# In-projection of a hybrid decoder layer: the column halves six k-steps apart, the woven steps spread evenly, the samples' states multiplied eight at a time

## The chip, the cores and the metric

The kernel runs on one core of a Trainium2 chip. The metric is the device time of one execution in microseconds (us). Its engines have a queue each and run them in order: TensorE (PE in the profile) multiplies, VectorE (DVE), ScalarE (ACT) and GpSimd (POOL) work on elements, SyncE (SP) issues most of the transfers.

## The reference

One step of a one-layer decoder with 520 token columns (512 of a prompt, 8 single new tokens, the samples) of width 2048:

```python
h = h + W_out [ GatedDeltaNet(x_n) ; MultiScalePool(x_n) ]     # x_n = RMSNorm(h)
h = h + SwiGLU(RMSNorm(h))
# W_in: 2048 -> [q | k | v | z | beta | decay | pool channels], q, k, v, z, pool 1024 wide each
def short_conv(buf, x, w):
    ext = jnp.concatenate([buf.astype(x.dtype), x], axis=1)
    T = x.shape[1]
    y = ext[:, 0:T] * w[0]
    for i in range(1, CONV_W):
        y = y + ext[:, i:i + T] * w[i]
    return jax.nn.silu(y), ext[:, -(CONV_W - 1):]
```

q, k and v go through the short convolution. The delta net has 8 heads of dimension 128: for the prompt its recurrence is computed in chunks, and each sample reads and updates its own state, a 128 x 128 matrix per head (`state_delta`, 8 samples x 8 heads). The second half of the width is pooled over windows of 2, 4, 8 and 16 tokens. Everything is float32.

## The kernel before, in words

The change lies in the first stage, the in-projection with the delta net and the pooling, up to about 580 us. The rest (out-projection and the feed-forward part) is not touched.

**Products.** `product` (L171 to L194 and its `step`) computes 128 output columns of W_in for all 520 tokens. There are 16 k-steps of 128 rows. Each float32 operand is split into two parts, hi and lo, and three matmuls stand for one: hi by hi (L171), hi by lo of the activations (L172), lo of the weights by hi (L173). The 520 tokens lie in two halves of 264 and 256 with an accumulator (mm) each, from a pool of three. So a product is 16 x 2 x 3 = 96 matmuls. Half 1 runs `SKEW` = 3 k-steps behind half 0: nine matmuls of half 0 alone, then both halves in turn, then nine of half 1 alone. As soon as a half is done it is evicted (by VectorE, L263 with the norm's factor), which frees its buffer for the next product.

**Weights.** A product's weights come in two granules of eight k-steps (512 KB). For each there is a load on SyncE's queue (raw, L134), the high part by ScalarE (hi, L138) and the low part by VectorE (lo, L140); three buffers of each serve in turn, so a granule can be split when the product before the last has read its own. These have a high priority in the queues, as have the evictions; apart from PE, whose order is that of the program (`manual_schedule`), a scheduler sets the order of the instructions on the engines.

**The weave.** The heads' own work (`keys`, `eliminate`, `delta`, `gate`, and the samples' and the pooling's steps) is cut into pieces by `yield n`: a generator yields after a piece, and runs on after n steps of the weave. `product` calls `weave.step()` 16 times. Before, there is none in the nine first matmuls; then one for every six matmuls, and in the last nine one for every three. So a piece is put in PE's queue between the product's matmuls, and what PE reads there has to be ready, or PE's whole queue waits.

**A head.** `delta` (two products per head, q and v) multiplies with a stored triangle (L871), does three elimination steps (L881 on PE, the result uu by VectorE in L883, the transposed factor xt_ by ScalarE in L873), and then four chunks in a chain: R from the state S (kp by PE in L908, R by VectorE in L910), W from R (L915), the new state S (L920 on PE; L923 or L925 on VectorE). The squares of queries and outputs are taken by ScalarE (L797, L934), the convolution y by VectorE (L748, L750). `eliminate` is a chain of 62 operations on VectorE for four heads at a time. The order of the products: four k tiles, four z tiles, and for each of four heads q and v; the same for the next four heads; then eight tiles of the pooling channels. The gates z are evicted into mixa and mixb.

**The samples.** In `sample_product` (L1000 on), a piece per four samples of a head: their states (s0, 256 KB, two buffers in turn, L1006 on SyncE's queue) are loaded, four matmuls multiply them with the key and query columns, each into its own 32 rows of one accumulator (L1009), and after four steps of the weave the next four follow: sixteen groups of four, in the products of the third to the last but one pool tile. The pieces of `sample_out` stand behind them (L1020, L1040, L1048).

Of the kernel before, what the change touches and what calls it, by code (L numbers as in the profile page):

```python
# [17 lines left out]
P = 128  # L18
D = 2048
KT = D // P  # L20
# [3 lines left out]
H = 8  # L24
# [11 lines left out]
    "ext": 2, "y": 1, "ys": 1, "g3": 3, "junk": 1, "ss": 2, "rr": 2, "nb": 1, "u": 1, "tm": 2, "xt_": 1, "uu": 2,  # L36
    "qts": 1, "fq": 2, "aq": 1, "vs": 1, "bt": 2, "tq": 1, "R": 2, "W": 2, "S": 2, "so": 2, "ro": 2, "s0": 2, "s2": 1, "kd": 4, "st": 2,
}
SKEW = 3
AHEAD = 2000  # L40


# [27 lines left out]
def decoder_kernel(ctx, tc, x_prompt, x_sample, state_delta, state_conv, state_pool, norm_mix, w_in,  # L70
# [4 lines left out]
    te, act, dve, pool, sp = nc.tensor, nc.scalar, nc.vector, nc.gpsimd, nc.sync  # L75
# [12 lines left out]
    def pst():  # L88
        return ps_dn.tile([P, 512], F32, tag="dn", name="dn")
# [34 lines left out]
    weave = Weave()  # L124
# [27 lines left out]
    def weights(view, K, parts=None):  # L152

        ng = -(-K // HG)
        sizes = [K // ng + (1 if i < K % ng else 0) for i in range(ng)]
        out = []
        k0 = 0
        for n in sizes:
            hi, lo = granule(view, k0, n, P, parts)
            for j in range(n):  # L160
                out.append((hi[:, j, :], lo[:, j, :]))
            k0 += n
        return out

    def accumulators():
        return [ps_mm.tile([P, c1 - c0], F32, tag="mm", name="mm") for c0, c1 in CHUNKS]

    def step(acc, w, hi, lo, ci, k):
        c0, c1 = CHUNKS[ci]
        wh, wl = w[k]  # L170
        te.matmul(acc[ci], wh, hi[k][:, c0:c1], start=(k == 0), stop=False)  # L171
        te.matmul(acc[ci], wh, lo[k][:, c0:c1], start=False, stop=False)  # L172
        te.matmul(acc[ci], wl, hi[k][:, c0:c1], start=False, stop=(k == len(w) - 1))  # L173

    def product(w, hi, lo, evict, skew=SKEW):

        K = len(w)
        acc = accumulators()

        def finish(ci):  # L180
            with tc.high_priority(offset=AHEAD):
                evict(ci, *CHUNKS[ci], acc[ci])

        for i in range(K + skew):
            if i < K:
                step(acc, w, hi, lo, 0, i)
                if i == K - 1:
                    finish(0)
            if i >= skew:
                step(acc, w, hi, lo, 1, i - skew)  # L190
                if i < K + skew - 1:
                    weave.step()
        finish(1)
        weave.step()  # L194

    def split(hi, lo, src):
        act.copy(hi, src)
        dve.tensor_tensor(lo, src, hi.bitcast(F32), op=ALU.subtract)  # L198
# [82 lines left out]
    with tc.tile_pool(name="ph0", bufs=2) as ph0, tc.high_priority(offset=10 * AHEAD), tc.manual_schedule():  # L281
# [173 lines left out]
        for i in range(17):  # L455
# [53 lines left out]
            ci, j = divmod(i, 8)  # L509
# [31 lines left out]
    with ExitStack() as p1:  # L541
# [4 lines left out]
        def d1tile(tag, shape, name, dtype=F32):  # L546
            return (pre if tag == "ext" else d1).tile(shape, dtype, tag=tag, name=name, bufs=BUFS[tag])
# [193 lines left out]
        def qkv_tile(sec, h, out, ext=None):  # L741
            t = sec * 8 + h
            if ext is None:
                ext = columns()
                product(weights(win_view(sec * 1024 + h * P), KT), xhk, xlk,
                        lambda ci, c0, c1, acc: to_columns(ext, t, ci, acc))
            y = d1tile("y", [P, SEQ], "y")
            dve.tensor_scalar(y, ext[:, 0:SEQ], cw(0, t), None, op0=ALU.mult)  # L748
            for i in range(1, 4):
                dve.scalar_tensor_tensor(y, ext[:, i:i + SEQ], cw(i, t), y, op0=ALU.mult, op1=ALU.add)  # L750
            act.activation(out, y, AF.Silu)
            pool.tensor_copy(ccp[:, :, t], ext[:, SEQ:SEQ + 3])
# [206 lines left out]
        smp = {}  # L959
# [40 lines left out]
        def sample_product(h):  # L1000

            if h == 0:
                smp["pk"] = pst()
            for hf in range(2):
                s0 = d1tile("uu", [P, 4, P], "s0")
                sp.dma_start(s0, state_delta[0, 4 * hf:4 * hf + 4, h].rearrange("b k v -> k b v"))  # L1006
                i = 2 * h + hf
                for j in range(4):
                    te.matmul(smp["pk"][32 * j:32 * j + 32, 0:P], smp["cols"][j][:, 32 * i:32 * i + 32], s0[:, j, :],  # L1009
                              start=(i == 0), stop=(i == 2 * H - 1))  # L1010
                yield 4

        def sample_out():
            take = smp["take"]
# [56 lines left out]
        def z_tile(h):  # L1071
            w = weights(win_view(3072 + h * P), KT)

            def evict(ci, c0, c1, acc):
                normed_out(mix[h][:, c0:c1], acc, c0, c1, c0)
                act.activation(mix[h][:, c0:c1], mix[h][:, c0:c1], AF.Silu)

            product(w, xhk, xlk, evict)
# [4 lines left out]
        def pool_tile(t, operands):  # L1083
# [6 lines left out]
            def evict(ci, c0, c1, acc):  # L1090
# [3 lines left out]
                else:  # L1094
                    normed_out(pe0[:, 15 + 256:15 + 512], acc, 264, NTOK, 264)

            product(w, xhk, xlk, evict)
            pool.tensor_copy(pcp[:, :, t], pe0[:, 512:527])
            cur = pe0
# [73 lines left out]
        for h in range(H):  # L1173
            weave.add(sample_product(h))
# [19 lines left out]
        order = [*range(8), 14, 15, 12, 13, 10, 11, 8, 9]  # L1194
# [3 lines left out]
        w = weights(w_out[0].rearrange("(k p) c -> p k c", p=P)[:, :, 8 * P:9 * P], KT)  # L1198
        acc_out = [ps_mm.tile([P, HALF], F32, tag="mm", name="mm") for _ in range(3)]

        def step_out(i, half):
            k = order[i]
            (wh, wl), c = w[k], slice(HALF * half, HALF * half + HALF)
            acc = acc_out[2 if half else k // 8]
            start, stop = i == 0 or not half and i == 8, i == KT - 1 or not half and i == 7
            te.matmul(acc, wh, xhk[k][:, c], start=start, stop=False)
            te.matmul(acc, wh, xlk[k][:, c], start=False, stop=False)
            te.matmul(acc, wl, xhk[k][:, c], start=False, stop=stop)

        for i in range(KT + SKEW):  # L1210
            if i == 14:
                weave.finish(1)
                for k in order[14:]:
                    split(xhk[k], xlk[k], mix[k])
            if i < KT:
                step_out(i, 0)
            if i >= SKEW:
                step_out(i - SKEW, 1)
            weave.step()
        mixed_t3 = mixed(2, 8), mixed(0, 2)  # L1220

# [438 lines left out]
    w = last.w  # L1660
# [32 lines left out]
    def add_to(i, half, acc):  # L1693
        x = mix[KT - 2 + i][:, HALF * half:HALF * half + HALF]
        dve.tensor_tensor(x, x, acc, op=ALU.add)

    def finish(i, half, acc):
        c = slice(HALF * half, HALF * half + HALF)
        add_to(i, half, acc)
        sq = p2.tile([P, NTOK], F32, tag="sq", name="sq")[:, c]  # L1700
        act.activation(sq, mix[KT - 2 + i][:, c], AF.Square)
        act.dma_start(h_d[KT - 2 + i][:, c], mix[KT - 2 + i][:, c])
        return sq, c
# [534 lines left out]
```

## Time and profile before

| | |
|---|---|
| median of 3 runs | 2142.9 us (2142.05 to 2143.71) |
| profiled execution | 2141.42 us, its span 2139.7 us |
| clock granted to TensorE over the span | 0.999 |
| TensorE busy | 2113.0 us |
| VectorE busy | 1774.5 us |
| ScalarE busy | 931.3 us |
| GpSimd busy | 434.9 us |

A row of the timeline gives start and duration in us, the engine, the line, the operation, output and inputs with their shapes, the number of instructions that it joins, and in brackets how long the engine stood idle before it and on what. Matmuls are pipelined: one lasts 0.28 us from start to end, but the next starts 0.12 us after it, so distances are taken between starts. In the waits, a row gives the engine and its line, the engine and line it waited for, the total in us, how often, and the longest. Start times in the text are those of the profiled execution, counted from the span's start. Places in a product are counted in its matmuls, of which there are 96.

### The profile page before, as it was taken

To read this page: it belongs to the slowest core of one execution; us is meant where nothing else is said; L and a number is where in the kernel's file an instruction comes from. 1 tells how busy PE (TensorE), PEld (TensorE's weight loads), DVE (VectorE), ACT (ScalarE), POOL (GpSimd) and SP (SyncE) were. 2 spreads that over 40 slices of the span, in tenths; PEclk is the share of its full clock that TensorE was granted. 3 is DMA by queue.
4 is the path that set the end of the run, shared out by engine and by line. 5 is a ranking of instruction groups with operands and counts; after the bars stand their busy time and mean duration, and the time that the engine had idled before them with its cause. 6 is when DMAs were issued, how large, how long until landed. Compare 5 with 4: busy or idle time off the path is not lost.

```text
span 2139.7 us, 42813 instructions
## 1 busy us (share of the span) xinstructions
PE 2113.0 (99%) x17685; PEld 2095.2 (98%) x17685; DVE 1774.5 (83%) x2616; ACT 931.3 (44%) x1369; POOL 434.9 (20%) x524
## 2 busy tenths in 40 slices
PE   8999999999999999999999999999999999999998
PEld 7999999999999999999999999999999999999998
DVE  7786767676699979888889889888877888888997
ACT  5533452442354454434334434434334434435444
POOL 2212320232012202332233233231011101001100
PEclk9999999999999999999999999999999999999999
DMA  8344434444445524655555656555448648348333
GB/s 277 101 129 107 122 98 122 116 112 111 129 133 159 162 87 131 175 179 173 168 173 176 181 168 182 144 145 152 122 127 249 192 134 261 106 120 267 90 108 120
DMA packets 477488, 321.29 MB, mean 150 GB/s; under 512 B 27692, under 2 KB 455365, under 8 KB 476765
## 3 DMA queue, kind: packets, MB, share of 16 engines
q1 hardware_dynamic: 459965, 263.49, 43.0%
q0 software_dynamic: 16016, 54.25, 7.9%
q8 instruction: 139, 2.28, 0.5%
q10 hardware_dynamic: 1312, 0.80, 0.1%
q14 instruction: 56, 0.46, 0.1%
HBM read 265.76 MB, written 53.40 MB: 149 GB/s over the span
## 4 chain that ended last, share of the span: by engine, by line
PE 85%; DVE 9%; issue 2%; ACT 2%; DMA 1%; POOL 1%; ACTq 0%; DVEq 0%; POOLq 0%; SPq 0%
PE dn L1280 21%; PE dn L1281 21%; PE dn L1282 21%; PE mm L171 6%; PE mm L173 5%; PE mm L172 5%; DVE lo L1274 1%; DVE lo L140 1%; PE dn L881 1%; ACT hi L1273 1%; DVE raw L1316 1%; DMA qk<-tok_d 1%; DVE xl L198 0%; DVE tm L847 0%; DVE u L849 0%
## 5 line engine op out<-in xcount | busy, mean ns | idle before, releaser
L1274 DVE TENSOR_TENSOR lo<-raw,hi 128x1024 fp32r<-128x1024 f32 (+1 forms) x422 | 543.2, 1307 | 70.3 <-ACT hi L1273 68.8
L1273 ACT CAST hi<-raw 128x1024 fp32r<-128x1024 f32 (+1 forms) x422 | 426.8, 1027 | 401.0 <-DVE raw L1316 226.5
L171 PE MATMUL mm<-xh,hi 128*128 128x256 f32 (+1 forms) x1280 | 376.7, 294 | 2.5 <-DVE mixa L263 2.5
L172 PE MATMUL mm<-xl,hi 128*128 128x256 f32 (+1 forms) x1280 | 361.6, 283 | 0.9 <-DVE xl L354 0.5
L173 PE MATMUL mm<-xh,lo 128*128 128x256 f32 (+1 forms) x1280 | 361.7, 283 | 0.4 <-DVE lo L140 0.4
L171 PEld LDWEIGHTS mm<-xh,hi 128*128 128x128 f32 x1280 | 241.1, 188 | 6.8 <-DVE mixa L263 3.2
L172 PEld LDWEIGHTS mm<-xl,hi 128*128 128x128 f32 x1280 | 241.6, 189 | 1.7 <-DVE xl L354 1.7
L173 PEld LDWEIGHTS mm<-xh,lo 128*128 128x128 f32 x1280 | 240.8, 188 | 0.6 <-DVE lo L140 0.6
L1282 PE MATMUL dn<-b21h,lo 128*128 128x260 f32 x598 | 169.3, 283 | 0.4 <-DVE lo L1274 0.4
L1281 PE MATMUL dn<-b21l,hi 128*128 128x260 f32 x598 | 169.4, 283 | 0.0
L1280 PE MATMUL dn<-b21h,hi 128*128 128x260 f32 x598 | 168.7, 282 | 0.0
L1282 PE MATMUL dn<-b11h,lo 128*128 128x260 f32 x590 | 167.0, 283 | 1.3 <-DVE lo L1274 1.3
L1316 DVE TENSOR_TENSOR raw<-raw 128x1024 f32<-128x1024 f32 (+1 forms) x130 | 166.2, 1278 | 2.2
L1281 PE MATMUL dn<-b11l,hi 128*128 128x260 f32 x590 | 167.1, 283 | 0.0
L1280 PE MATMUL dn<-b11h,hi 128*128 128x260 f32 x590 | 166.6, 282 | 0.0
L1486 POOL TENSOR_TENSOR mixa<-mixa 128x520 f32<-128x520 f32 x22 | 50.4, 2290 | 568.7 <-DVE mixa L1480 568.7
L1467 ACT ACTIVATE sg<-sg 128x260 f32<-128x260 f32 x88 | 37.0, 422 | 264.9 <-DVE sg L1466 264.9
L1280 PE MATMUL dn<-T1h,hi 128*128 128x260 f32 x534 | 151.9, 284 | 0.0
L1281 PE MATMUL dn<-T1l,hi 128*128 128x260 f32 x534 | 151.5, 284 | 0.0
L138 ACT CAST hi<-raw 128x1024 fp32r<-128x1024 f32 (+2 forms) x86 | 87.2, 1015 | 142.3 <-PE mm L172 135.4
L140 DVE TENSOR_TENSOR lo<-raw,hi 128x1024 fp32r<-128x1024 f32 (+2 forms) x87 | 102.1, 1175 | 52.9 <-ACT hi L138 51.4
L1282 PE MATMUL dn<-T1h,lo 128*128 128x260 f32 x512 | 144.3, 282 | 0.0
(671 smaller groups left out, 6695.3 us busy)
## 6 DMA issues: line engine op xcount, KB each, us to landing
raw<-in_w_gate_up_dram SPq DMA_DIRECT2D x134, 512.0 KB
raw<-in_w_in_dram SPq DMA_DIRECT2D x79, 512.0 KB
a_d<-mixa SPq DMA_DIRECT2D x22, 1040.0 KB
raw<-in_w_down_dram SPq DMA_DIRECT2D x48, 448.0 KB
mixb<-in_w_gate_up_dram SPq DMA_DIRECT2D x41, 512.0 KB
raw<-in_w_out_dram SPq DMA_DIRECT2D x25, 512.0 KB
raw<-in_w_down_dram SPq DMA_DIRECT2D x24, 512.0 KB
sg<-in_w_down_dram SPq DMA_DIRECT2D x14, 448.0 KB
```

The lines of the kernel that those rows point to most:

```text
L138: act.copy(hi[:, r], raw[:, r])
L140: dve.tensor_tensor(lo[:, r], raw[:, r], hi[:, r].bitcast(F32), op=ALU.subtract)
L171: te.matmul(acc[ci], wh, hi[k][:, c0:c1], start=(k == 0), stop=False)
L172: te.matmul(acc[ci], wh, lo[k][:, c0:c1], start=False, stop=False)
L173: te.matmul(acc[ci], wl, hi[k][:, c0:c1], start=False, stop=(k == len(w) - 1))
L1273: act.copy(hi, raw)
L1274: dve.tensor_tensor(lo, raw, hi.bitcast(F32), op=ALU.subtract)
L1280: te.matmul(acc, wh[:, k, :], xf[:, k, :], start=start and k == 0, stop=False)
L1281: te.matmul(acc, wh[:, k, :], xg[:, k, :], start=False, stop=False)
L1282: te.matmul(acc, wl[:, k, :], xf[:, k, :], start=False, stop=stop and k == wh.shape[1] - 1)
L1316: dve.tensor_tensor(r[name], r[a], r[b], op=op)
L1486: pool.tensor_tensor(q[:, 4:8:2, :], q[:, 1:4:2, :], q[:, 0:2, :], op=ALU.subtract)
```

## The change

Three things are changed, all in the in-projection. `SKEW` goes from 3 to 6: half 1 of each product runs six k-steps behind half 0, so that 18 matmuls of half 0 stand alone at the start and 18 of half 1 at the end. The weave's steps no longer hang on half 1's k-steps: the product's 32 pairs of half and k-step are written as one list, and every second of them is followed by a step, so one for every six matmuls from matmul 6 to 96; there are 16 as before. The samples' states are loaded for a whole head at a time, two tiles of four samples, and multiplied in one group of eight; the group comes every eight steps (after six the first time), and the next head's loads are issued behind it. The out-projection's own loop used the same constant and keeps 3 (`lag`).

```diff
-SKEW = 3
+SKEW = 6
...
-        for i in range(K + skew):
-            if i < K:
-                step(acc, w, hi, lo, 0, i)
-                if i == K - 1:
-                    finish(0)
-            if i >= skew:
-                step(acc, w, hi, lo, 1, i - skew)
-                if i < K + skew - 1:
-                    weave.step()
-        finish(1)
-        weave.step()
+        order = [(ci, i - skew * ci) for i in range(K + skew) for ci in range(2) if 0 <= i - skew * ci < K]
+        for n, (ci, k) in enumerate(order):
+            step(acc, w, hi, lo, ci, k)
+            if k == K - 1:
+                finish(ci)
+            if n % 2:
+                weave.step()
...
             if h == 0:
                 smp["pk"] = pst()
+                load_states(0)
+                yield 6
+            for hf in range(2):
+                i = 2 * h + hf
+                for j in range(4):
+                    te.matmul(smp["pk"][32 * j:32 * j + 32, 0:P], smp["cols"][j][:, 32 * i:32 * i + 32],
+                              smp["s0"][hf][:, j, :], start=(i == 0), stop=(i == 2 * H - 1))
+            if h + 1 < H:
+                load_states(h + 1)
+                yield 8
+
+        def load_states(h):
+            smp["s0"] = []
             for hf in range(2):
                 s0 = d1tile("uu", [P, 4, P], "s0")
                 sp.dma_start(s0, state_delta[0, 4 * hf:4 * hf + 4, h].rearrange("b k v -> k b v"))
-                i = 2 * h + hf
-                for j in range(4):
-                    te.matmul(smp["pk"][32 * j:32 * j + 32, 0:P], smp["cols"][j][:, 32 * i:32 * i + 32], s0[:, j, :],
-                              start=(i == 0), stop=(i == 2 * H - 1))
-                yield 4
+                smp["s0"].append(s0)
```

The lines of the changed kernel stand four lower in the part that matters (L881 becomes L877, L915 becomes L911, the states' L1009 becomes L1005, their load L1006 becomes L1015).

More of the change, by code (lines that the diff above doesn't have):

```diff
@@ L1208, in step_out @@
             te.matmul(acc, wl, xhk[k][:, c], start=False, stop=stop)
-        for i in range(KT + SKEW):
+        lag = 3
+        for i in range(KT + lag):
             if i == 14:
@@ L1216, in decoder_kernel @@
                 step_out(i, 0)
-            if i >= SKEW:
-                step_out(i - SKEW, 1)
+            if i >= lag:
+                step_out(i - lag, 1)
             weave.step()
```

## The prediction

> **What bounds it now.** First the page's busy times and its chain of waits:
>
> ```profile
> PE 2113.0 (99%) x17685; PEld 2095.2 (98%) x17685; DVE 1774.5 (83%) x2616; ACT 931.3 (44%) x1369; POOL 434.9 (20%) x524
> PE 85%; DVE 9%; issue 2%; ACT 2%; DMA 1%; POOL 1%; ACTq 0%; DVEq 0%; POOLq 0%; SPq 0%
> ```
>
> PE (TensorE) has work 99% of the time and carries 85% of the chain. The change leaves the number of its matmuls as it is, so it can win only where PE stands still or pays for a switch, and lose only where PE gets a new wait. Next the busy time by stage of the in-projection, and PE's waits from 60 to 606 us:
>
> ```profile
> core 0: us, PE busy (x) PEld busy (x) DVE busy (x) ACT busy (x) POOL busy (x), PEclk, DMA share, GB/s
> 100.00:160.00 60.00, 57.18 (x471) 56.34 (x469) 50.24 (x122) 19.70 (x33) 10.74 (x23) 1.00 0.48 125
> 160.00:500.00 340.00, 338.40 (x2912) 335.13 (x2913) 235.30 (x537) 136.91 (x302) 83.31 (x163) 1.00 0.41 111
> 570.00:606.00 36.00, 34.88 (x289) 34.42 (x288) 30.43 (x65) 18.77 (x33) 1.53 (x3) 1.00 0.31 88
> ```
> ```profile
> engine line waited for: us in total, times, longest us
> PE mm L171 <- DVE mixa L263: 2.5, 3, 1.2
> PE dn L881 <- DVE uu L883: 0.7, 1, 0.7
> PE dn L881 <- ACT xt__2114 L873: 0.7, 1, 0.7
> PE dn L881 <- ACT xt__4928 L873: 0.5, 1, 0.5
> PE dn L1040 <- DVE sc_u L1037: 0.3, 1, 0.3
> ```
>
> The clock is 1.00 in every stage. There is little to win: 2.5 us in three z products, where the next product needs the accumulator that VectorE has not yet read, 1.9 us in three elimination steps of a head, and 0.3 us near the end. The long stage with the heads, 160 to 500, has 1.6 us of idle PE in 340, though VectorE is busy for 235: the weave already fits, with little slack at each place, as the rows below show.
>
> **The sample's states.** Now a group of four states:
>
> ```profile
> 514.08 0.28 PE L173 MATMUL mm<-xh,lo 128*128 128x256 f32 x1
> 514.28 0.42 PE L1009 MATMUL dn<-s,utf 128*32 128x128 f32 x8
> 514.64 0.39 PE L171 MATMUL mm<-xh,hi 128*128 128x264 f32 x1
> 514.87 0.29 PE L172 MATMUL mm<-xl,hi 128*128 128x264 f32 x1
> 514.99 0.29 PE L173 MATMUL mm<-xh,lo 128*128 128x264 f32 x1
> ```
>
> From L173 to L173 there are 0.91 us; the product's own three starts, 0.12 apart (514.87 to 514.99), would take 0.36, so a group adds 0.55. It is two sets of four side by side. Eight states are two sets more in the same group, each about 0.135: 0.36 from the group's start to L171 is two sets and the way out, and the way out is taken at 0.09, which leaves 0.135 for a set. So a group of eight adds 0.55 + 0.27 = 0.82, and eight of these in place of sixteen of 0.55 give 8 x (1.10 - 0.82) = **-2.2 us** (bounds -3.3, if the added sets cost nothing, to 0, if each pair of groups costs as much as before).
>
> **Its loads.** The pair of tiles for the next head can be loaded only when the whole group has read the last pair; before, one of the two was always under way. On SyncE's queue, around the sixth pool tile (s0 are the states, raw the weight granules of the seventh and eighth pool tile), stood:
>
> ```order
> L134 DMA raw_6982<-in_w_pool_dram 128x2x256
> L1006 DMA s0_6805<-in_state_delta_dram 128x4x128
> L1006 DMA s0_6837<-in_state_delta_dram 128x4x128
> L1006 DMA s0_6898<-in_state_delta_dram 128x4x128
> L134 DMA raw_7060<-in_w_in_dram 128x8x128
> L134 DMA raw_7066<-in_w_in_dram 128x8x128
> L1006 DMA s0_6928<-in_state_delta_dram 128x4x128
> ```
>
> and now
>
> ```order
> L1015 DMA s0_6716<-in_state_delta_dram 128x4x128
> L1015 DMA s0_6718<-in_state_delta_dram 128x4x128
> L134 DMA raw_7058<-in_w_in_dram 128x8x128
> L1015 DMA s0_6814<-in_state_delta_dram 128x4x128
> L134 DMA raw_7064<-in_w_in_dram 128x8x128
> L1015 DMA s0_6816<-in_state_delta_dram 128x4x128
> ```
>
> The second half of head 3's pair stands behind both weight loads, each of which waits until VectorE has split an earlier granule. The same four transfers in the trace of before, and the traffic from 531 to 539 in slices of 0.2 us:
>
> ```profile
> 531.40 0.37 SPq L1006 DMA_DIRECT2D s<-in_state_delta_dram  x1
> 531.83 1.68 SPq L134 DMA_DIRECT2D raw<-in_w_in_dram  x2
> 534.84 0.37 SPq L1006 DMA_DIRECT2D s<-in_state_delta_dram  x1
> GB/s 0 0 0 0 0 0 0 118 136 77 261 343 336 277 328 333 335 320 348 364 289 287 284 261 292 297 307 294 302 300 292 302 282 253 184 85 21 0 0 10
> ```
>
> 1.5 MB (256, 512, 512 and 256 KB) flow at about 300 GB/s until 538, 6.6 us after the first issue. In the changed kernel all four are issued from 2.3 us after matmul 66 of the fourth pool tile, where the split of the granule begins (a hi and a lo, rows below), and are through at 2.3 + 6.6 = 8.9; the next group stands 48 matmuls behind the group at that place: 0.82 + 48 x 0.12 = 6.6, and its second half 0.4 later. PE would wait 8.9 - 7.0 = 1.9 us, once; at the other pairs nothing stands between. I take **+1.6** (0 if the last transfer overtakes, 2.4 if it lands last of all). The Trainium skill, page DMA: Bandwidth & Descriptors, section Anatomy of one DMA, gives a transfer as some 2.0 us fixed and bytes over 436 GB/s; by that the four would take 5.6 us and the wait would be an estimated 0.9 us. The traffic above stays at about 300, so the rows decide.
>
> **Later accumulators.** Half 0 now ends at matmul 75 of 96 instead of 84, and the next product asks for its buffer at 21 instead of 12: 42 matmuls, 5.0 us, in place of 24, 2.9 us. The three waits on mixa end there. But between 100 and 160 VectorE is busy 50 of 60 us with the elimination, whose chain has to be through for the first head; what z no longer waits for is waited for there. **+0.5** (-2.5, all of the waits gone, to +2).
>
> Weights: granule 1's buffer comes free at matmul 66 instead of 57 and the next product reads it from 30 instead of 39: 60 matmuls, 7.2 us, for a hi of 1.05 and a lo of 1.23 us (rows below). Hidden: 0.
>
> **The weave nine matmuls earlier.** Before, the first step came after matmul 15, now after 6; at most places of a head that is 9 x 0.12 = 1.08 us earlier in the product. VectorE's queue isn't earlier by that. For one head, the first elimination step's result and the step that reads it:
>
> ```profile
> 225.16 0.55 DVE L883 SCALAR_TENSOR_TENSOR uu<-dn,utf 96x384 f32<-96x384 f32 x1
> 226.11 0.27 PE L881 MATMUL dn<-uu,xt__2900 128*64 128x64 f32 x1
> ```
>
> uu is there at 225.71, behind a queue of VectorE that runs without a pause; PE comes to it at 226.11 and would now come at 225.03: a wait of 0.68. **A**: five heads (1, 2, 3, 5, 6) x 0.65 = **+3.2** (0 to 5, if the queue is ahead by then or if the signal takes 0.2 more). Heads 4 and 7 hold two of the three waits on L881 and get a queue in another order: **-0.6** (-1.3 to +1).
>
> The next place is the second chunk of a head. VectorE's queue before (S the state, lo the weights' low part, ext and ccs the eviction, R the right side that PE multiplies in L915, y the convolution):
>
> ```order
> L140 TENSOR_TENSOR lo_2686<-raw_2684,hi_2685 128x1024
> L955 SCALAR_TENSOR_TENSOR mixa_100<-mixb_101,prm_105,mixa_100 128x512
> L923 COPY S_2616<-dn_2614 128x128
> L910 SCALAR_TENSOR_TENSOR R_2637<-dn_2635,negc_668,vs_2561 128x128
> L263 TENSOR_TENSOR ext_2456<-mm_2470,rb_113 128x256
> L263 TENSOR_TENSOR ccs_112<-mm_2470,rb_113 128x8
> L263 TENSOR_TENSOR ext_2456<-mm_2471,rb_113 128x256
> L925 SCALAR_TENSOR_TENSOR S_2663<-S_2616,egl_670,dn_2661 128x128
> L748 TENSOR_SCALAR y_2668<-ext_2456,prm_105 128x512
> L140 TENSOR_TENSOR lo_2857<-raw_2855,hi_2856 128x1024
> L750 SCALAR_TENSOR_TENSOR y_2668<-ext_2456,prm_105,y_2668 128x512
> L910 SCALAR_TENSOR_TENSOR R_2709<-dn_2707,negc_668,vs_2561 128x128
> ```
>
> and now:
>
> ```order
> L919 COPY S_2607<-dn_2605 128x128
> L140 TENSOR_TENSOR lo_2686<-raw_2684,hi_2685 128x1024
> L259 TENSOR_TENSOR ext_2456<-mm_2470,rb_113 128x256
> L259 TENSOR_TENSOR ccs_112<-mm_2470,rb_113 128x8
> L906 SCALAR_TENSOR_TENSOR R_2628<-dn_2626,negc_668,vs_2552 128x128
> L951 SCALAR_TENSOR_TENSOR mixa_100<-mixb_101,prm_105,mixa_100 128x512
> L259 TENSOR_TENSOR ext_2456<-mm_2471,rb_113 128x256
> L921 SCALAR_TENSOR_TENSOR S_2663<-S_2607,egl_670,dn_2661 128x128
> L744 TENSOR_SCALAR y_2668<-ext_2456,prm_105 128x512
> L140 TENSOR_TENSOR lo_2857<-raw_2855,hi_2856 128x1024
> L746 SCALAR_TENSOR_TENSOR y_2668<-ext_2456,prm_105,y_2668 128x512
> L906 SCALAR_TENSOR_TENSOR R_2700<-dn_2698,negc_668,vs_2552 128x128
> ```
>
> The first R now has the weights' lo and the eviction between it and S; the second R keeps its place behind lo and y. Their times in before, on ScalarE, VectorE and PE:
>
> ```profile
> 230.03 1.05 ACT L138 CAST hi<-raw 128x1024 fp32r<-128x1024 f32 x1 [4.12 <-PE mm L172]
> ```
> ```profile
> 231.12 1.23 DVE L140 TENSOR_TENSOR lo<-raw,hi 128x1024 fp32r<-128x1024 f32 x1 [1.33 <-ACT hi L138]
> 232.26 0.75 DVE L955 SCALAR_TENSOR_TENSOR mixa<-mixb,prm,mixa 128x512 f32<-128x512 f32 x1
> ...
> 233.94 0.35 DVE L910 SCALAR_TENSOR_TENSOR R<-dn,negc,vs 128x128 f32<-128x128 f32 x1 [0.73 <-PE dn L908]
> 234.31 0.42 DVE L263 TENSOR_TENSOR ext<-mm,rb 128x256 f32<-128x256 f32 x1
> 234.65 0.17 DVE L263 TENSOR_TENSOR ccs<-mm,rb 128x8 f32<-128x8 f32 x1
> ...
> 236.94 1.22 DVE L140 TENSOR_TENSOR lo<-raw,hi 128x1024 fp32r<-128x1024 f32 x1
> 238.07 0.75 DVE L750 SCALAR_TENSOR_TENSOR y<-ext,prm,y 128x512 f32<-128x512 f32 x1
> 238.74 0.34 DVE L910 SCALAR_TENSOR_TENSOR R<-dn,negc,vs 128x128 f32<-128x128 f32 x1
> ```
> ```profile
> 234.82 0.38 PE L915 MATMUL dn<-R,uu 128*128 128x128 f32 x2
> 239.88 0.38 PE L915 MATMUL dn<-R,uu 128*128 128x128 f32 x2
> ```
>
> **B**, first R: hi starts when PE lets its buffer go, 9 matmuls later: 231.11. So lo starts at 232.20, ext at 233.34 (1.14 later, as 231.12 to 232.26), ccs 0.34 later, R at 233.82, done at 234.17. PE comes to L915 six matmuls earlier (84 instead of 90), 234.10, and needs some 0.2 for the signal: 0.28, in eight heads **+2.2** (0 to 4). **C**, second R: in the next product everything of VectorE's keeps its distance from the product's start, so R is there at 239.08; L915 comes at 18 instead of 27, 238.80: 0.28 and 0.07 for the signal, in seven heads **+2.5** (0 to 3.5).
>
> **The end.** From 570 to 606 VectorE is busy 30.4 of 36 us; the last sample steps come nine to 21 matmuls earlier, which takes the 0.3 wait on L1040 and a little of the queue behind it: **-0.7** (-1.5 to +1, if the lo of the last pool tile's weights comes late).
>
> **Sum**: -2.2 + 1.6 + 0.5 + 3.2 - 0.6 + 2.2 + 2.5 - 0.7 = +6.5 us. On the profiled execution's 2141.4 that is 2147.9; the median of the runs is 1.5 above it, so 2149.4.
>
> **Rivals.**
> 1. *The queue gives way.* VectorE has 105 idle us in the 340 of the heads; S and the squares come earlier as well, and if the queue gets ahead of PE once, A, B and C are nothing. For it: only a few tenths of a us decide each. Against it: the rows before uu and R stand back to back. Then -2.2 - 2.5 - 0.6 - 0.7 + 0 = -6.0: 2136.9, or with the load's 1.6, 2138.5. Faster; chance 0.27.
> 2. *Half of it.* A alone or B and C alone: 6.5 less 3.2 or 4.7, 2144.7 to 2146.2, no change to be told. Chance 0.27. (The states' loads in time, alone, would leave 6.5 - 1.6 = 4.9, 2147.8, still slower.)
> 3. *Weights late.* If the lo of a granule gets behind two evictions and the pool tile's chain, the window of 7.2 us could be short where pool granules hold a buffer; one such wait of 1 us in each of the last four products would be +4 on the sum, 2153.4. Within the forecast's side; it decides where the window's 7.2 us are less than queue and split.
>
> **Numbers.** Slower by the sum and by rival 3: 0.46. 0.2%, 4.3 us, is about what a measurement of this kernel can tell from no change, so slower begins at 2147.2 and faster ends at 2138.6. The range takes in rival 1's 2136.9 and, upward, A, B and C at 0.9 us more each than taken with rival 3 half true (6.5 + 2.7 + 2 = 11.2, 2154.1): 2136.5 to 2154.5. The forecast's own range is 2147 to 2154.5.
>
> **What would show it.** In the changed kernel's waits: L877 (the old L881) on uu some five times at 0.6, L911 (old L915) on R about fifteen times at 0.3, and L1005 on s0 once at 1 to 2 us; no wait on mixa's eviction; PE's sample groups eight at 0.8 us. Each of the R rows in VectorE's queue should end after PE has come. I am wrong if PE's idle time between 160 and 500 doesn't grow from 1.6 us to some 8; if it shrinks, rival 1 holds.

## The result, and the profile after

The changed kernel takes 2158.69 us (median of 4 runs, 2157.07 to 2160.22) beside 2142.78 for the kernel before: a ratio of 1.0075 (95% interval 1.0062 to 1.0087). It is slower by 16 us, where 6.5 us were forecast. The profiled execution took 2157.3 us, its span is 2155.6.

First the page's busy times and the top of its chain:

```profile
PE 2117.4 (98%) x17685; PEld 2098.6 (97%) x17685; DVE 1771.2 (82%) x2616; ACT 937.6 (43%) x1373; POOL 439.0 (20%) x524
PE 77%; DVE 7%; ACT 2%; issue 1%; DMA 0%; POOL 0%; DVEq 0%; SPq 0%; ACTq 0%; POOLq 0%
```

The work is the same, and VectorE isn't busier than before. The time went into waits. The same stages as in the prediction:

```profile
core 0: us, PE busy (x) PEld busy (x) DVE busy (x) ACT busy (x) POOL busy (x), PEclk, DMA share, GB/s
100.00:160.00 60.00, 56.28 (x453) 55.66 (x452) 46.58 (x122) 23.78 (x31) 7.52 (x18) 0.97 0.42 114
160.00:500.00 340.00, 328.86 (x2797) 322.38 (x2797) 225.86 (x521) 133.78 (x299) 85.85 (x162) 1.00 0.40 109
570.00:606.00 36.00, 36.00 (x332) 34.98 (x331) 27.20 (x59) 13.91 (x22) 0.65 (x4) 1.00 0.45 126
```

In the stretch of the heads, 160 to 500, PE is idle for 11.1 us instead of 1.6, and in 100 to 160 the granted clock is 0.97. PE's waits from 60 to 606 us say for what:

```profile
PE dn L892 <- ACT vT L747: 4.4, 6, 1.5
PE dn L877 <- DVE uu L879: 4.2, 6, 2.8
PE mm L171 <- DVE mixa L259: 3.3, 2, 2.5
PE dn L911 <- DVE R L906: 2.2, 10, 0.3
PE dn L1005 <- DMA s<-in_state_delta_dram: 1.2, 1, 1.2
PE mm L173 <- DVE lo L140: 0.4, 1, 0.4
PE dn L911 <- DVE pw L1116: 0.3, 1, 0.3
```

Only waits of 0.15 us or more are listed. Three of the rows were forecast: uu, R and the states' load. The first was not: the transposition of vT. And mixa's wait, which was to go, grew from three waits of 2.5 in all to two of 3.3. Where the time is lost is best read from the starts of the products, compared with those of before (each from its profiled execution, in us; the products are numbered from 0 and a stretch runs from start to start; the first head, number 0, is multiplied in products 10 and 11, the heads 1 to 3 lie in 11 to 18, the heads 4 to 7 in 26 to 34, the states in 34 to 39):

| stretch | 2 to 11 | 11 to 18 | 18 to 26 | 26 to 34 | 34 to 39 | the rest |
|---|---|---|---|---|---|---|
| forecast | +0.5 | heads together +7.3 | 0 | | -0.6 | -0.7 |
| changed kernel | +5.2 | +6.0 | 0.0 | +5.9 | -2.0 | +0.7 |

The 0.3 us wait on L1040, which the forecast counted to the end (-0.7), lay in product 38, so it belongs to the stretch 34 to 39.

**A head.** In the third head's product, VectorE, ScalarE and PE:

```profile
231.01 0.70 DVE L771 STREAM_TRANSPOSE bt<-mixb 128x512 f32<-128x512 f32 x1
231.64 0.71 DVE L746 SCALAR_TENSOR_TENSOR y<-ext,prm,y 128x512 f32<-128x512 f32 x1
232.27 0.55 DVE L879 SCALAR_TENSOR_TENSOR uu<-dn,utf 96x384 f32<-96x384 f32 x1
232.74 0.74 DVE L746 SCALAR_TENSOR_TENSOR y<-ext,prm,y 128x512 f32<-128x512 f32 x1
```
```profile
233.51 0.63 ACT L747 ACTIVATE vT<-y 128x512 f32<-128x512 f32 x1 [2.33 <-DVE y L746]
```
```profile
232.96 0.65 PE L877 MATMUL dn<-uu,xt__2891 128*64 128x64 f32 x8 [0.26 <-DVE uu L879]
234.19 0.44 PE L892 MATMUL dn<-ident,vT 128*128 128x128 f32 x2 [0.58 <-ACT vT L747]
```

uu now has VectorE before the last pass of the convolution, so it comes earlier than forecast, and PE waits 0.26 for it. But the pass that was put behind it ends at 233.48, the silu at 234.14, and the transposition, which stands in PE's queue right behind L877, waits 0.58. In the kernel before, the same rows had room:

```profile
225.28 0.63 ACT L751 ACTIVATE vT<-y 128x512 f32<-128x512 f32 x1 [1.03 <-DVE y L750]
```
```profile
226.11 0.68 PE L881 MATMUL dn<-uu,xt__2900 128*64 128x64 f32 x8
226.72 0.66 PE L896 MATMUL dn<-ident,vT 128*128 128x128 f32 x4
```

vT was there at 225.91, 0.81 before PE needed it. Two deadlines 0.6 us apart hung on one queue, and the forecast priced one.

**The elimination.** The load of its input nb, behind a weight load on SyncE's queue, and VectorE's first operation of it, before and after:

```profile
108.05 0.40 SPq L134 DMA_DIRECT2D raw<-in_w_in_dram  x1
108.49 0.58 SPq L786 DMA_DIRECT2D gcb<-gcr_d  x1
109.74 0.53 SPq L837 DMA_DIRECT2D nb<-nd_d  x1
```
```profile
113.98 0.20 DVE L847 TENSOR_TENSOR tm<-nb,u 64x31 f32<-64x31 f32 x1 [0.38 <-DMA nb<-nd_d]
```
```profile
109.92 0.37 SPq L782 DMA_DIRECT2D gcb<-gcr_d  x1
110.81 0.41 SPq L134 DMA_DIRECT2D raw<-in_w_in_dram  x1
111.46 0.53 SPq L833 DMA_DIRECT2D nb<-nd_d  x1
```
```profile
117.84 0.20 DVE L843 TENSOR_TENSOR tm<-nb,u 64x31 f32<-64x31 f32 x1 [6.33 <-DMA nb<-nd_d]
```

nb is asked for 1.7 us later and takes 6.4 us instead of 4.2, so VectorE stands idle for 6.3 us and its chain of 62 operations begins 3.9 us late. The rest of it follows from there: z's eviction waits among those operations, and PE for the eviction. In the first head it is again VectorE's queue that passes the delay on. The convolution of its queries follows the elimination there, so their load (qk) is issued at 158.34 instead of 154.21, ScalarE's squares of them come later, and uu stands in the queue behind their sums (ss):

```profile
165.97 0.17 DVE L931 TENSOR_SCALAR ss<-ss 128x4 f32<-128x4 f32 x1 [1.82 <-ACT junk L930]
166.05 0.75 DVE L746 SCALAR_TENSOR_TENSOR y<-ext,prm,y 128x512 f32<-128x512 f32 x1
166.71 0.55 DVE L879 SCALAR_TENSOR_TENSOR uu<-dn,utf 96x384 f32<-96x384 f32 x1
```
```profile
167.31 0.39 PE L877 MATMUL dn<-uu,xt__2105 128*64 128x64 f32 x3 [2.82 <-DVE uu L879]
```

In the kernel before, the same sums were taken at 161.10, uu was there at 163.16, and PE, which came at 163.58, didn't wait for it.

### The profile page after: what moved, and what is told of

Its sections match the earlier page's. It is cut to its first block, busy times and chain, and to the rows that moved or that the text cites. A ratio compares the mean times of both kernels' runs of the same rounds, so it can differ in the third digit from the quotient of the medians.

```text
span 2155.6 us, 42811 instructions
## 1 busy us (share of the span) xinstructions
PE 2117.4 (98%) x17685; PEld 2098.6 (97%) x17685; DVE 1771.2 (82%) x2616; ACT 937.6 (43%) x1373; POOL 439.0 (20%) x524
## 4 chain that ended last, share of the span: by engine, by line
PE 77%; DVE 7%; ACT 2%; issue 1%; DMA 0%; POOL 0%; DVEq 0%; SPq 0%; ACTq 0%; POOLq 0%
PE dn L1286 21%; PE dn L1287 21%; PE dn L1288 21%; PE mm L171 4%; PE mm L172 3%; PE mm L173 3%; DVE lo L1280 1%; DVE lo L140 1%; ACT hi L1279 1%; DVE raw L1322 1%; DVE y L746 1%; ACT hi L138 0%; PE dn L911 0%; PE mm L1286 0%; PE mm L1287 0%
## 5 line engine op out<-in xcount | busy, mean ns | idle before, releaser
L173 PE MATMUL mm<-xh,lo 128*128 128x256 f32 (+1 forms) x1280 | 362.2, 283 | 0.8 <-DVE lo L140 0.8
L173 PEld LDWEIGHTS mm<-xh,lo 128*128 128x128 f32 x1280 | 242.0, 189 | 1.2 <-DVE lo L140 1.2
L1286 PE MATMUL dn<-B22h,hi 128*128 128x260 f32 x504 | 143.5, 285 | 0.2 <-ACT hi L1279 0.2
L1287 PE MATMUL dn<-B22l,hi 128*128 128x260 f32 x504 | 143.1, 284 | 0.0
```

What stands on the lines that cost most here:

```text
L1286: te.matmul(acc, wh[:, k, :], xf[:, k, :], start=start and k == 0, stop=False)
L1287: te.matmul(acc, wh[:, k, :], xg[:, k, :], start=False, stop=False)
```

## The experiments

All are compared with the kernel before, run on the same chip beside them. The stretches are those of the table above.

**The states alone.** The kernel before, with `load_states` and the group of eight:

```diff
+            for hf in range(2):
+                i = 2 * h + hf
...
+                              smp["s0"][hf][:, j, :], start=(i == 0), stop=(i == 2 * H - 1))
```

> The kernel before with only the states multiplied eight at a time. Theory 1 (the weave's places are the cost): -2 to -3.5 us from eight fewer switches; the one late pair of loads costs up to 1.4 if it is late here too; 2139.5 to 2142. Theory 2 (the later accumulator and weight buffers are the cost): the same. If the states were the cost: 2148 or more.

Measured: 2139.64 (before 2143.01), ratio 0.9984 (0.9974 to 0.9993). The stretch of the states is 2.2 us shorter, with 0.8 us of waits for their loads in it. This part of the change is a gain, and the version is faster than both kernels. By the way: in its profiled execution the elimination began at 116.66, though every engine's queue there is as in before, whose execution has 113.98; 0.7 of this is a later start of everything, the rest a gcb load that took 5.7 us instead of 3.9. So one execution says the place of the loss in 2 to 11, but its size only to some 2 us.

**SKEW alone, even spacing alone, the whole change at the old places.**

```diff
-SKEW = 3
+SKEW = 6
```

> The kernel before with only SKEW 6 in the in-projection, in the old loop, so that the first step of the weave stands after matmul 24 instead of 15 and the last six of it three matmuls apart. Theory 1 (places too early): no wait on vT or uu grows, the three evictions' 2.5 us go; 2138 to 2144. Theory 2 (buffers free at 66 instead of 57, lo and evictions ahead of R): waits on R at 0.3 to 0.6 in each head, and later elimination; 2148 to 2156.

```diff
-        for i in range(K + skew):
...
+            if n % 2:
+                weave.step()
```

> The kernel before with only the evenly spread weave (a step after matmul 6, 12, ... 96), SKEW 3, states in fours. Theory 1: about all of the loss, waits on vT and uu of 1.1 us in five heads, elimination late: 2154 to 2160. Theory 2: little of it, under 2147.

```diff
-            if n % 2:
+            if n > 3 and (n % 2 == 0 or n > 28):
                 weave.step()
```

> The changed kernel (SKEW 6, states in eights) with the weave's steps at the old matmuls: 15, 21, ... 87, 90, 93, 96. Theory 1: the waits on vT and uu go and the elimination is as early as before; 2137 to 2143. Theory 2: still slow, 2150 or more, with waits on R.

| kernel | median, before | ratio (95%) | 2 to 11 | 11 to 18 | 26 to 34 |
|---|---|---|---|---|---|
| SKEW 6, old loop (first step at 24) | 2152.68, 2143.01 | 1.0042 (1.0027 to 1.0057) | +3.2 | +3.7 | +2.4 |
| even spacing, SKEW 3 | 2153.67, 2143.01 | 1.0050 (1.0035 to 1.0065) | +2.1 | +6.7 | +4.6 |
| whole change, old places | 2159.28, 2143.01 | 1.0074 (1.0059 to 1.0089) | +6.1 | +4.4 | +5.8 |

So theory 1, that the early places alone are the cost, falls: with the old places the change is no faster. SKEW alone costs too, as theory 2 had it, but theory 2 alone falls as well, since the even spacing costs without SKEW. With the old places the waits are others:

```profile
PE dn L904 <- DVE S L919: 5.4, 8, 0.8
PE dn L877 <- ACT xt__2114 L869: 3.0, 1, 3.0
PE dn L877 <- DVE uu L879: 2.4, 2, 2.2
PE dn L892 <- ACT vT L747: 2.3, 4, 0.6
```

S, once a head, now comes behind the weights' lo, which starts nine matmuls later, and the first eviction. SKEW moves the lo and the first eviction by nine matmuls against the product, the spacing moves the head's pieces by nine; each by itself sets one against the other, and each time it is another link of the head's chain that PE waits for. That suggested the third theory: what costs is the order on the queues, not the places.

**The order on VectorE's queue.** The changed kernel, with the transposition of vT a piece later; with R first; and with both:

```diff
-                if it == 1:
+                if it == 2:
                     vtp = pst()
```

> The changed kernel with the transposition of vT one piece (12 matmuls) later, behind the third elimination step. Theory 1 (vT, behind uu and the convolution on VectorE and the silu on ScalarE, is what PE waits for): the six waits of 4.4 us on L892 go and nothing stands in their place: 2154 to 2156. Rival: PE then waits the same time for uu or for vs, since VectorE is the bound there: 2157 to 2160.

```diff
+                    with tc.high_priority(offset=2 * AHEAD):
-                    dve.scalar_tensor_tensor(Rt, kp[:, 0:P], negc[:, c, h:h + 1], vs[:, ck(c)],
-                                             op0=ALU.mult, op1=ALU.add)
+                        dve.scalar_tensor_tensor(Rt, kp[:, 0:P], negc[:, c, h:h + 1], vs[:, ck(c)],
+                                                 op0=ALU.mult, op1=ALU.add)
```

> The changed kernel with R given the highest priority, so that VectorE has it ahead of the eviction in the first product and ahead of y in the second. Theory 1 (the order on VectorE's queue makes the waits of B and C): the ten or more waits on R, 2.5 us idle and some 0.1 each for the restart, go: 2154.5 to 2156.5. Rival (PE comes too early for S and the weights' lo, whatever the order): 2157 to 2160.

> Both edits of the two runs before it. Theory 1: the two gains add, 2150 to 2153.5. Rival (VectorE's queue as a whole is the bound): 2155 or more.

| kernel | median, before | ratio (95%) | 2 to 11 | 11 to 18 | 26 to 34 |
|---|---|---|---|---|---|
| vT later | 2156.41, 2142.25 | 1.0064 (1.0049 to 1.0079) | +7.5 | +4.2 | +4.4 |
| R first | 2153.09, 2142.25 | 1.0047 (1.0031 to 1.0064) | +7.9 | +3.0 | +2.3 |
| both | 2147.71, 2142.25 | 1.0028 (1.0018 to 1.0037) | +6.9 | +1.0 | -0.4 |

In the waits of the kernel with both, vT and R are gone:

```profile
PE dn L877 <- DVE uu L879: 5.1, 7, 3.5
PE mm L171 <- DVE mixa L259: 3.6, 3, 2.5
PE dn L1006 <- DMA s<-in_state_delta_dram: 1.3, 1, 1.3
PE mm L173 <- DVE lo L140: 1.0, 1, 1.0
```

The heads lose 0.7 us instead of 11.9. The gains are more than the sum: 2.3 and 5.6 from the changed kernel's median for each alone, 11.0 for both. In the heads' stretches alone they nearly add: 3.4, 6.7 and 11.3. The stretch 2 to 11 is 1.8 to 2.7 us longer in these three executions than in the changed kernel's, which takes as much from each gain. vT alone took away its own wait and met others behind it, 3.8 us of waits in L911 by way of ro, pw and R itself where the changed kernel has 2.5. R alone gained more than its waits' 2.2 us: its 0.9 us a head are the two waits with the restart. With the heads repaired, what is left stands in 2 to 11.

**Three matmuls instead of nine.** SKEW 3 and states in fours, each step of the weave three matmuls earlier than before:

```diff
+            if n % 2 and 2 < n < 28 or 27 < n < 31:
+                weave.step()
```

> The kernel before (SKEW 3, states in fours) with the weave's steps three matmuls earlier: 12, 18, ... 84, 87, 90, 93. Theory 1 (each place has a slack, in before 0.40 us for uu, 0.53 and 0.80 for the two R, 0.81 for vT; what is moved by 0.36 us doesn't wait): 2142 to 2145. Rival (any other spacing makes the scheduler set worse queues, as with the old places under SKEW 6): 2148 or more.

Measured: 2145.08 (before 2142.25), ratio 1.0012 (1.0003 to 1.0022); 2 to 11 +0.4, the heads +1.9 and +0.9. That is far less than a third of the 11.3 us that nine matmuls cost the heads in the even spacing, but not zero, and just above the forecast. PE loses time at two places in each head: at S, whose slack of 0.31 in before (there at 233.21, read at 233.52) wasn't on the list, and at the second R, for which it now stands about 0.1 us though its slack was read as 0.80.

**The gcb load.** In the changed kernel the fourth head's gcb, which the keys' chain needs on the way to nb, stands behind the second head's four stores on SyncE's queue, and ahead of them in before. It is put ahead again; and this with both repairs of the heads:

```diff
+            with tc.high_priority(offset=ahead):
-            sp.dma_start(gcb, gcr_d[h:h + 1, :].broadcast_to([P, SEQ]))
+                sp.dma_start(gcb, gcr_d[h:h + 1, :].broadcast_to([P, SEQ]))
...
-            _, dm = decay(h)
+            _, dm = decay(h, AHEAD if h == 3 else 0)
```

> The changed kernel with the fourth head's gcb load given a high priority, so that it stands ahead of the second head's four stores on SyncE's queue again, as before the change. Theory 1 (that load, 3.9 us late, makes the elimination start 3.9 us late, and the first head then waits for it): the elimination starts 2 to 4 us earlier, the eleventh product's start is 1 to 3 us behind instead of 5.2; 2155 to 2157. Rival (the later evictions and weights of SKEW 6 delay the elimination): no change, 2158 to 2160.

> The changed kernel with all three repairs: R first, the transposition of vT a piece later, the gcb load ahead. Theory 1: the gains add, 2143 to 2146, about as the kernel before. Rival (the spacing itself, by way of VectorE as a whole, costs several us): 2147 or more.

Measured: 2161.53 (before 2141.73), ratio 1.0090 (1.0075 to 1.0105); and 2149.54 (before 2141.73), ratio 1.0038 (1.0025 to 1.0051). Theory 1 misses both times. In the first, the fourth head's dm comes 2.1 us earlier (98.94 instead of 101.08), but ScalarE then has its exponential ahead of the third head's squares, and nb is asked for at 111.56, as in the changed kernel (111.46). The elimination begins at 118.35. With all three repairs it is no faster than with the two. The gcb load isn't the cause that can be taken away by itself.

**SKEW 6 in the z products alone.** The states in eights, the old places, and

```diff
-            product(w, xhk, xlk, evict)
+            product(w, xhk, xlk, evict, 6)
```

in `z_tile`, with the gcb load in its old place:

> The kernel before with the states in eights, and SKEW 6 in the eight z products alone, at the old places of the weave, with the gcb load in its old place. No head is woven into those products. Theory (VectorE's elimination is the bound there, and what z no longer waits for is waited for by the first head): within 1 us of the states alone, 2138.5 to 2141. Rival (the z products' three waits are the accumulator's alone): 2 to 3 us faster than the states alone, 2136 to 2138.

Measured: 2143.81 (before 2141.73), ratio 1.0008 (0.9998 to 1.0018). It is slower than the states alone, by 3.7 us in the profiled executions and by 5.4 in the medians, each against its own runs of before, so both expectations miss: the waits don't go, one of 4.5 us takes the place of the longest, since the elimination begins at 119.52, the latest of all. Yet from there to product 11 it is 59.8 us, as in before. All fourteen executions share this: product 11 starts 59.7 to 60.3 us after the elimination's first operation in the six kernels that have SKEW 3 in the products of q and v then (before, 113.98 and 173.80; the states alone, even spacing, three matmuls, this one and the next), and 61.2 to 64.2 in the eight with SKEW 6 there. SKEW 6 in the z products doesn't enter.

**The change from the heads on.** The changed kernel with R first and vT later, where the first ten products that use the loop keep SKEW 3 and the old places:

```diff
+        calls.append(1)
+        early = len(calls) <= 10
+        if early:
+            skew = 3
...
-            if n % 2:
+            if n > 3 and (n % 2 == 0 or n > 28) if early else n % 2:
                 weave.step()
```

> The changed kernel with R first and the transposition of vT a piece later, and with the first ten products that run in this way (up to those into which the first head is woven) as before: SKEW 3 and the old places; from the next on the change is whole. Theory (the loss is the elimination's late start and first head, and the two queue places R and vT, and nothing else): the stretch to the first head costs nothing, the heads up to 1.5 us, the states give 2: 2140 to 2143, within 0.1% of before. Rival (the loss of 5 to 7 us by the first head comes back later in another place, since VectorE is the bound): 2146 or more.

Measured: 2141.98 (before 2142.46), ratio 0.9998 (0.9989 to 1.0007), no difference. 2 to 11 costs 0.1, the heads 0.8 and -0.4, the states give 1.9. Its waits:

```profile
PE mm L171 <- DVE mixa L265: 2.6, 3, 1.2
PE dn L883 <- DVE uu L885: 1.4, 5, 0.3
PE dn L1012 <- DMA s<-in_state_delta_dram: 1.3, 1, 1.3
```

So the 16 us are found: the stretch up to the first head, and the two queue places of vT and R in the heads. Nothing comes back later. SKEW 6 and the even spacing from the heads on, with the queues mended, bring nothing; the states' part is what gains, and alone it is the fastest version, 2.9 us ahead of this one in the medians, each against its own runs of before.

## Why the prediction was right or wrong

**Right**: slower, and in the heads by waits on PE that its queue's order makes, B and C at the places named. B and C were 0.28 and 0.35 us a head; the distances between the matmuls around L911 grew by 0.46 and about 0.41, the restart of the pipeline included. Priority for R took both away. The 0.2 us that B adds for the signal stand in no row; in the waits on VectorE and ScalarE PE starts 0.05 to 0.15 us after the result's end.

The paired load was taken at 1.6: one wait of 1.2, at head 3's second half as forecast, 1.4 with the restart. That it came so near is in part luck: the first of the four loads was issued 0.4 us after matmul 66 (547.42), not 2.3, and from there to PE's release (555.30) it took 7.9 us, not 6.6. The traffic did stay at about 300 GB/s (269 to 356 in steps of 0.4 us from 549.4 to 553.8). The figures of the Trainium skill, page DMA: Bandwidth & Descriptors, section Anatomy of one DMA, by which the prediction had an estimated 5.6 us, are for transfers that GpSimd issues; these are SyncE's, so the 7.9 us are no test of them.

A group of eight costs 0.78 us where 0.82 was worked out (the bound of -3.3 for added sets that cost nothing should have been 8 x 0.55 = -4.4):

```profile
537.60 0.29 PE L173 MATMUL mm<-xh,lo 128*128 128x264 f32 x1
537.81 0.65 PE L1005 MATMUL dn<-s,utf 128*32 128x128 f32 x16
538.39 0.39 PE L171 MATMUL mm<-xh,hi 128*128 128x264 f32 x1
538.61 0.29 PE L172 MATMUL mm<-xl,hi 128*128 128x264 f32 x1
538.74 0.29 PE L173 MATMUL mm<-xh,lo 128*128 128x264 f32 x1
```

From L173 to L173 1.14 us, less 0.36.

**Wrong, first step: "Later accumulators", +0.5 (-2.5 to +2).** It measured +5.2. The step took the elimination's start as given and looked only at who waits for its end. But its start hangs on the keys' chain, in which each head's piece crosses four queues (SyncE's gcb, VectorE's dm, ScalarE's exponential and squares, GpSimd's power, SyncE's stores, nb), and the change re-orders them. 3.8 us come from the start (3.9 later, 0.1 of it before product 2), and 1.4 from the way on to product 11 (61.2 instead of 59.8): L877 waits 2.8 for uu in the first head, where L881 didn't, and most of the 1.4 is that PE reaches that step nine matmuls (1.1 us) earlier in the product, so that as much more of it is left when the wait ends. The sentence that what z no longer waits for is waited for by the first head was right; the start was the term left out. That the later nb load does it isn't shown by an edit, only by the rows: where the weight load stood 1.6 us or more ahead of nb, nb took 4.2 to 4.5 us in five of six kernels, and 5.4 in one; where it stood 0.65 ahead, 6.4 to 7.0 in all six. The two kernels in between don't fit a rule by the distance alone: 6.3 us at 1.39 (the old places), and 7.6, the longest, at 1.06 (SKEW 6 in z alone). Which of the four queues would have to be mended stays open; putting the weight load behind nb wasn't tried on the chip.

**Wrong, second step: A, "five heads x 0.65".** It measured 1.0 a head with the restarts, for uu and vT's transposition together; with R first and vT later 0.3 of it is left, for uu. So uu cost half of what was forecast, and vT the rest. The wait was worked out from VectorE's queue of before, in which uu is last; in the changed queue uu is ahead, and y, and with it vT, is late. vT's slack of 0.81 in before was in the trace and less than the 1.08 by which PE came earlier, and wasn't looked at. **Heads 4 and 7, -0.6**, came to +0.25, read in the kernel with R first: head 4 gained 0.7, as its wait in L881 went, and head 7 cost 1.0, as the others did, with the longest wait on vT (1.5 in the changed kernel).

**Wrong in size: the states.** Their stretch gave 2.0 net, not 0.6. Eight groups save 2.6 (8 x 2 x 0.55 less 8 x 0.78), and the load costs 1.4. The rest is the wait on L1040, which is gone: with the even spacing and with the three matmuls, where the states are in fours, the stretch gained 0.8 and 0.7, 0.6 of it in L1040's product. So what **the end** priced at -0.7 came as -0.6, in product 38; why the rest of the kernel took 0.7 longer is open.

Rival 1 (the queue gives way) didn't hold: only with R and vT set by hand does it. Rival 3 (weights late in the last products) didn't show; the one wait on lo, 0.4 us, is in a z product.

## What to carry to other kernels

When work is moved earlier on the engine that is the bound, list every operand that it reads there, with the slack of each in the trace, not the one that ends last now: two that are 0.6 us apart on the same queue are two waits, and mending one shows the next. A piece that is placed by hand and a block with a high priority (a split, an eviction) that another constant moves have to be looked at together. And a long chain on another engine is priced from its start: what feeds it crosses other queues, and the change moves those as well.

## What the runs showed of the hardware that was not expected

The wait of 2.5 us from 122.0 to 124.6 in the changed kernel slowed what came behind it. Its windows of 3.41 us, laid at the clock's own steps:

```profile
121.85:125.26 3.41, 0.87 (x7) 0.70 (x6) 3.24 (x9) 0.72 (x2) 0.00 (x0) 1.00 0.22 66
125.26:128.68 3.42, 3.42 (x18) 3.42 (x17) 3.32 (x8) 1.07 (x2) 0.00 (x0) 0.50 0.54 153
128.68:132.09 3.41, 3.41 (x30) 3.41 (x29) 3.13 (x9) 0.36 (x1) 0.00 (x0) 1.00 0.56 159
162.81:166.22 3.41, 1.68 (x15) 1.47 (x13) 1.55 (x4) 1.87 (x9) 0.59 (x2) 1.00 0.86 211
166.22:169.64 3.42, 2.33 (x22) 2.25 (x23) 3.24 (x10) 1.65 (x2) 1.51 (x2) 1.00 0.19 40
```

After a window in which PE was busy for 0.87 us the granted clock is 0.50 for the next whole window, 18 recorded matmuls in place of 30. The longer wait, 2.8 us from 164.5 to 167.3, falls on two windows, 1.68 and 2.33 busy, and the clock stays. Where R is first, 1.30 us of work in a window was too little:

```profile
122.90:126.30 3.40, 1.30 (x11) 1.30 (x11) 3.26 (x8) 1.32 (x2) 0.00 (x0) 1.00 0.12 27
126.30:129.70 3.40, 3.40 (x18) 3.40 (x17) 3.30 (x8) 0.46 (x2) 0.00 (x0) 0.50 0.46 136
```

So in these runs the line lies between 1.3 and 1.7 us of work in 3.41, and whether a wait of 2.5 to 3 us meets it depends on where it falls. A halved window has room for 1.7 us less of PE's work, an estimate from 18 matmuls in place of 30. It happened in eight of the twelve experiments' profiles, in all with SKEW 6 before the first head; in four of them the clock stays at 0.50 for two windows (6.83 us). In the seven kernels that have a halved window in the first head, after 163, the stretch from the elimination to product 11 takes 62.2 to 64.2 us, and it may be part of that. In the changed kernel and with SKEW 6 in z alone, which have it at 125 only, it takes 61.2 and 59.8: there, where PE waits for VectorE's elimination anyhow, no cost of it is shown. The Trainium skill, page TensorE: Matmul & The Clock Gate, Part 1, describes a free-running window of 3413 ns by whose activity the clock is halved or restored. The trace agrees in the length, 3.41 us, and shows here how little work in one is too little: in all the traces with a halved window, the windows with at most 1.31 us of work are followed by one, and none with 1.68 or more is, except where the clock was at 0.50 already.
